# A chunked state-space scan on one core: three kinds of element-wise steps moved from GpSimd to VectorE

## The chip, the cores and the metric

The kernel runs on one core of a Trainium2 chip. The metric is the device time of one execution in microseconds; of several runs the median counts. The core's engines work side by side, each through its own queue in order: TensorE (PE in the profile, its weight loads PEld) multiplies matrices, VectorE (DVE) and ScalarE (ACT) do element-wise work, GpSimd (POOL) does element-wise work and issues some DMAs, SyncE (SP) issues DMAs.

## What is computed

One step of a hybrid decoder layer, for a prompt of 1024 positions and for 8 sequences that each decode one position. The layer projects the normalized input, runs a short causal convolution, a Mamba-2 scan in chunks of 128 positions and a pooling branch, projects back, and ends with a convolutional feed-forward block. The change touches the scan, the decode step of the scan's state, and the grouped norm behind it. The reference of the scan, cut down:

```python
acum = jnp.cumsum(dtc * a.reshape(G, R), axis=2)
decay = jnp.exp(jnp.where(causal, diff, -jnp.inf))
cb = jnp.einsum('bclgn,bcsgn->bclsg', cc, bc)
mix = cb[..., None] * decay * dtc[:, :, None]
y_diag = jnp.einsum('bclsgr,bcsgrp->bclgrp', mix, xc)
chunk_states = jnp.einsum('bclgn,bclgr,bclgrp->bcgrpn', bc, decay_to_end * dtc, xc)
chunk_decay = jnp.exp(acum[:, :, -1])
h = chunk_decay * h + chunk_states          # from chunk to chunk
y_off = jnp.einsum('bclgn,bcgrpn,bclgr->bclgrp', cc, h_in, jnp.exp(acum))
y = y_diag + y_off
```

Behind it come `y = (y + d_skip * x) * silu(z)` and a root-mean-square norm over each of four channel groups.

## The kernel before

Channels lie on the 128 partitions and positions along the free dimension. Every large product is made of three matmuls, since weights and inputs are split into a high and a low part: ScalarE makes a weight tile's high part (L140), and VectorE or GpSimd the low part (L141). A projection tile is a run of such matmuls in three column blocks (L159 to L161).

The scan has 24 heads, done in two halves of 12 (`q` = 0 and 1), each over 8 chunks (`c`). Here they are called the first and the second scan. Neither runs alone: the function `between`, called at each column block of a projection, hands out the scan's steps at a set rate, so the first scan lies between the matmuls of the projections that yield the second half's inputs, and the second between those of the gates. The order on each engine is then set by a scheduler that places the instructions by its own estimates of their durations.

One scan step `c` is made of three functions:

- `decay` loads the cumulated decays by DMA into `mix` and `ce`, clamps `mix` on VectorE (L538), and takes 12 exponentials of `mix` and one of `ce` on ScalarE (all at L188, a helper's line). Then `ce` is multiplied by C (L553): this is C with its exponentials, 128x768 elements, for every chunk but the first.
- `turn` transposes B and x on TensorE (L565, L574), multiplies B by C (L571), copies x to `xd` (L575), masks the product to `cb` (L576), scales `xd` for the state (L578) and multiplies `mix` by `cb` (L583, two instructions of 128x768), these four on VectorE.
- `apply` computes the chunk's state on TensorE (L597), multiplies the old state by its decay (L606, 128x384) and adds the two on VectorE (L610), multiplies `mix` with `xd` (L620) and `ce` with the old state (L630) on TensorE, and adds the skip on VectorE (L638).

One PSUM bank, `pM`, serves both the state product and the next transposition of B, so L565 waits for L610. The buffers of `mix`, `ce` and the state are doubled.

The decode step of a tile (`sample_tile`, L653 to L682) runs on GpSimd alone: it loads a state of 128x512 (L666), updates it (L670 to L673), stores it (L674) and reduces it with C by six halving additions (L675, L680). Of its 12 tiles, three are handed out between the two scans, four within the second, five behind it. `sample` ties each to the latest decay instruction of the scan (`self.pl`, L606), so that it is issued behind it.

Gates are applied on VectorE (L698, L700). `group_norm` takes squares on ScalarE (L710, L712) and adds them (L714, 128x1056, twice per group): on GpSimd for the first two groups, which fall within the second scan, on VectorE for the other two. `group_scale` sums over partitions on TensorE (L721) and scales on VectorE (L730).

In the first scan GpSimd also makes the low parts of the projection weights (L141, `self.lo_eng`); in the second VectorE does. The convolution of a projected tile (L516, three instructions of 128x1056) is VectorE's.

Of the kernel before, what the change touches and what calls it, by code (L numbers as in the profile page):

```python
# [13 lines left out]
ALU = mybir.AluOpType  # L14
# [4 lines left out]
P = 128  # L19
# [56 lines left out]
class Kernel:  # L76
    def __init__(self, ctx, tc, d):
        self.ctx, self.tc, self.nc, self.d = ctx, tc, tc.nc, d
        nc = self.nc
        pool = lambda name, bufs=1, **kw: ctx.enter_context(tc.tile_pool(name=name, bufs=bufs, **kw))  # L80
        self.const = pool("const")
        self.wpool = pool("weights")
        self.big = pool("big", 30)
        self.dram = pool("scratch", 1, space=DRAM)

        self.cst = self.const.tile([P, NCONST], F32, name="cst")
        self.mat = self.const.tile([P, NMAT], F32, name="mat")
        self.conv_st = self.const.tile([P, 16, 35], F32, name="conv_st")
        self.ones = self.const.tile([P, P], F32, name="ones")
        nc.vector.memset(self.ones, 1.0)  # L90
        self.zero = self.const.tile([P, P], mybir.dt.bfloat16, name="zero")
        nc.vector.memset(self.zero, 0.0)
        self.eps = self.const.tile([P, 1], F32, name="eps")
        nc.gpsimd.memset(self.eps, EPS)
        self.ident = self.mat[:, M_ID : M_ID + P]
        self.uid = 0
        self.lo_eng = nc.vector
        self.hooks = []
        self.pl = None
        self.tab = self.set = None  # L100
        self.table_set(EXPLN)

# [426 lines left out]
    def decay(self, q, c):  # L529

        nc = self.nc
        h0 = 12 * q
        mix = self.ph.tile([P, 12, P], F32, tag="mix", name=self.nm("mix"), bufs=2)
        src = lambda h, n, p: self.acd[c : c + 1, h * P : (h + n) * P].partition_broadcast(p)
        nc.sync.dma_start(mix.rearrange("p r l -> p (r l)"), src(h0, 12, P))
        hs = c * NH + h0

        nc.vector.scalar_tensor_tensor(  # L538
            out=mix, in0=self.acl[:, hs : hs + 12].unsqueeze(2).broadcast_to([P, 12, P]), scalar=80.0, in1=mix,
            op0=ALU.subtract, op1=ALU.max,  # L540
        )
        ce = None
        if c > 0:
            ce = self.ph.tile([P, 6, P], F32, tag="ce", name=self.nm("ce"), bufs=2)
            for g in range(2):
                rows = slice(64 * g, 64 * g + 64)
                nc.sync.dma_start(ce[rows].rearrange("p r l -> p (r l)"), src(h0 + 6 * g, 6, 64))
        for r in range(12):
            self.tables(mix[:, r], mix[:, r], AF.Exp, bias=self.acl[:, hs + r : hs + r + 1], scale=-1.0)
        if c > 0:  # L550
            self.tables(ce, ce, AF.Exp, scale=-1.0)
            cc = self.ctl[q][:, c * P : (c + 1) * P]
            nc.gpsimd.tensor_tensor(out=ce, in0=ce, in1=cc.unsqueeze(1).broadcast_to([P, 6, P]), op=ALU.mult)  # L553
        return mix, ce

    def turn(self, q, c, mix):
# [31 lines left out]
    def apply(self, q, c, mix, ce, xd, bT):  # L588

        nc = self.nc  # L590
        cols = slice(c * P, (c + 1) * P)
        h = self.hst.get(q)
        halves = [slice(0, 64), slice(64, 128)]
        pys = [self.bank("pY") for _ in range(2)]
        pst = self.bank("pM")
        for g, rows in enumerate(halves):
            nc.tensor.matmul(  # L597
                pst[rows, :384], bT[:, rows], xd[:, 1, 6 * g : 6 * g + 6].rearrange("p r x -> p (r x)"),
                start=True, stop=True,
            )  # L600
        h1 = self.ph.tile([P, 384], F32, tag="h", name=self.nm("h"), bufs=2)
        if c == 0:
            nc.scalar.activation(h1, pst[:, :384], AF.Copy)
        else:
            by_head = lambda t: t.rearrange("p (r x) -> p r x", x=64)
            self.pl = nc.gpsimd.tensor_tensor(  # L606
                out=by_head(h1), in0=by_head(h),
                in1=self.cd[:, c, q].unsqueeze(2).broadcast_to([P, 6, 64]), op=ALU.mult,
            ).ins
            nc.vector.tensor_tensor(out=h1, in0=h1, in1=pst[:, :384], op=ALU.add)  # L610
        self.hst[q] = h1
        if c == NCH - 1:
            nc.sync.dma_start(self.d["ssm_p"][q], h1)

        for g in range(2):
            for i in range(3):
                o = slice(i * P, (i + 1) * P)
                for j, out in enumerate(halves):
                    r = 6 * g + 2 * i + j
                    nc.tensor.matmul(  # L620
                        pys[g][out, o], xd[:, 0, r, :], mix[:, r, :], start=(i == 0), stop=(c == 0 and i == 2),
                        skip_group_check=True,
                    )

        for i in range(3 if c > 0 else 0):
            o = slice(i * P, (i + 1) * P)
            for j, out in enumerate(halves):
                r = 2 * i + j
                for g, rows in enumerate(halves):
                    nc.tensor.matmul(  # L630
                        pys[g][out, o], h[rows, r * 64 : (r + 1) * 64], ce[rows, r, :], start=False, stop=(i == 2),
                        skip_group_check=True,
                    )
        for g in range(2):
            for i in range(3):
                k = 6 * q + 3 * g + i
                t = self.xs[k][:, cols]
                nc.vector.scalar_tensor_tensor(  # L638
                    out=t, in0=t, scalar=self.c("dsk", k), in1=pys[g][:, i * P : (i + 1) * P],
                    op0=ALU.mult, op1=ALU.add,  # L640
                )
# [65 lines left out]
    def group_norm(self, g):  # L707
        nc = self.nc
        sq = [self.short(SW, "sq") for _ in range(2)]
        nc.scalar.activation(sq[0], self.xs[3 * g], AF.Square)  # L710
        for i in range(1, 3):
            nc.scalar.activation(sq[1], self.xs[3 * g + i], AF.Square)  # L712
            eng = nc.gpsimd if g < 2 else nc.vector
            eng.tensor_tensor(out=sq[0], in0=sq[0], in1=sq[1], op=ALU.add)  # L714
        self.later(2, lambda: self.group_scale(g, sq))

    def group_scale(self, g, sq):
# [36 lines left out]
    def ssd_phase(self):  # L754
        nc, d = self.nc, self.d
# [18 lines left out]
        def ssd_tasks(q):  # L774
            dec, trn = {}, {}

            def start():
                dec[0] = self.decay(q, 0)

            def step(c):  # L780
                if c >= 0:
                    self.apply(q, c, *dec.pop(c), *trn.pop(c))
                if c + 1 < NCH:
                    trn[c + 1] = self.turn(q, c + 1, dec[c + 1][0])
                if c + 2 < NCH:
                    dec[c + 2] = self.decay(q, c + 2)
                if c == -1 and q == 0:
                    self.sample_bc(q)
                if q == 1 and c in (0, 2, 4, 6):
                    sample(3 + c // 2)  # L790

            queue.append(start)
            for c in range(-1, NCH):
                queue.append(lambda c=c: step(c))

        def sample(i):
            with self.behind(self.pl):
                self.sample_tile(i // 6, i)

        self.lo_eng = nc.gpsimd  # L800
        for n in range(1, 6):
# [8 lines left out]
        for i in range(3):  # L810
            queue.append(lambda i=i: sample(i))
# [808 lines left out]
```

## Time and profile before

| | us |
|---|---|
| median of 3 runs | 1403.05 |
| the runs | 1397.98, 1403.05, 1403.52 |
| the profiled execution | 1399.9 |
| its span on the core | 1398.1 |

The profile is of one execution. Its page gives each engine's busy time and share of the span; a table of stretches gives the same for parts of the span, with the mean clock that TensorE was granted as a share of full speed. In the list of waits a row reads: the engine and line that waited, the engine and line that ended the wait, the total in us, how many times, the longest. In a timeline a row has start and duration in us, engine, line, operation, output and inputs, shape, and in brackets the idle time ahead of it with what ended it. A row of a group has the number of instructions, their busy time in us, the mean duration in ns, and the engine's idle time ahead of them.

### The profile page before, as it was taken

Reading aid. Unit: us, or ns where it says so; the run is one execution under the profiler, and the core shown is the slowest. Engines: PE = TensorE matmul, PEld = TensorE weight load, DVE = VectorE, ACT = ScalarE, POOL = GpSimd, SP = SyncE. Lnnn points to the kernel's source line nnn. Section 1 sums busy time; section 2 is a strip of 40 time slices with the busy share of each in tenths; the row PEclk is TensorE's granted clock in tenths of the full one; section 3 lists DMA queues with packets and bytes.
Section 4 is the critical chain, followed back from the end, with each engine's and each line's share of the span. In section 5 each row is a group of like instructions: output and inputs, shape, how many; then the busy total and the mean of one; then the engine's idle time right before and its main releaser. Section 6 shows DMA issues by size and latency. Waiting matters only on the chain.

```text
span 1398.1 us, 26823 instructions
## 1 busy us (share of the span) xinstructions
PE 1359.6 (97%) x10360; PEld 1312.8 (94%) x10360; DVE 986.9 (71%) x1501; ACT 701.3 (50%) x1408; POOL 496.8 (36%) x656
## 2 busy tenths in 40 slices
PE   8999999988999999999979999999999999999997
PEld 7799879977799999999979999999999999999997
DVE  6575899588864685755789867776776787567743
ACT  6346774655645451312447545554555465444451
POOL 4233466888578202122321222221222223214122
PEclk9999999999999999999989999999999999999999
DMA  7031235252331258665586877777777869657513
GB/s 250 1 109 39 87 121 173 81 162 98 95 105 63 73 187 280 224 199 187 151 199 151 210 202 197 199 191 200 176 179 199 204 214 324 225 180 238 179 54 121
DMA packets 117819, 228.08 MB, mean 163 GB/s; under 512 B 19884, under 2 KB 37116, under 8 KB 117692
## 3 DMA queue, kind: packets, MB, share of 16 engines
q1 hardware_dynamic: 73772, 130.21, 29.7%
q0 software_dynamic: 27056, 70.22, 20.0%
q10 hardware_dynamic: 16864, 25.95, 5.6%
q8 instruction: 81, 1.33, 0.4%
q14 instruction: 46, 0.38, 0.1%
HBM read 169.64 MB, written 45.15 MB: 154 GB/s over the span
## 4 chain that ended last, share of the span: by engine, by line
PE 82%; DVE 7%; DMA 3%; POOL 3%; issue 3%; ACT 2%; DVEq 0%; SPq 0%; POOLq 0%; ACTq 0%
PE g L1120 30%; PE g L1307 15%; PE g L160 10%; PE g L161 10%; PE g L159 10%; DVE wop L141 1%; DVE mix L583 1%; PE pY L620 1%; DVE xd L578 1%; POOL st L680 1%; DMA s<-wup 1%; DVE xs L516 1%; DVE xs L638 1%; PE pY L630 1%; DVE mix L538 1%
## 5 line engine op out<-in xcount | busy, mean ns | idle before, releaser
L1120 PE MATMUL g<-op,wop 128*128 128x258 f32 x3696 | 448.0, 284 | 3.9 <-ACT op L1045 3.7
L1120 PEld LDWEIGHTS g<-op,wop 128*128 128x128 f32 x3696 | 446.9, 190 | 4.7 <-ACT op L1045 4.1
L140 ACT ACTIVATE wop<-raw 128x512 fp32r<-128x512 f32 (+1 forms) x208 | 125.9, 608 | 228.1 <-PE g L161 134.3
L1307 PE MATMUL g<-op,wop 128*128 128x258 f32 x1848 | 224.9, 283 | 1.6 <-ACT op L210 0.8
L159 PE MATMUL g<-hh,wop 128*128 128x344 f32 x696 | 226.3, 325 | 0.0
L160 PE MATMUL g<-hl,wop 128*128 128x344 f32 x696 | 225.6, 324 | 0.0
L161 PE MATMUL g<-hh,wop 128*128 128x344 f32 x696 | 225.1, 323 | 0.0
L1307 PEld LDWEIGHTS g<-op,wop 128*128 128x128 f32 x1848 | 222.5, 189 | 2.6 <-ACT op L210 1.0
L141 DVE TENSOR_TENSOR wop<-raw,wop 128x512 fp32r<-128x512 f32 (+1 forms) x186 | 139.2, 752 | 88.6 <-ACT wop L140 86.6
L140 ACT ACTIVATE wop<-s 128x512 fp32r<-128x512 f32 (+1 forms) x136 | 83.6, 620 | 140.2 <-PE g L1307 51.9
L159 PEld LDWEIGHTS g<-hh,wop 128*128 128x128 f32 x696 | 132.5, 190 | 1.2 <-issue 1.1
L161 PEld LDWEIGHTS g<-hh,wop 128*128 128x128 f32 x696 | 132.3, 190 | 1.2 <-issue 1.2
L160 PEld LDWEIGHTS g<-hl,wop 128*128 128x128 f32 x696 | 132.2, 190 | 0.5 <-issue 0.4
L1100 POOL DMA_DIRECT2D s<-s x44 | 37.7, 857 | 249.8 <-DMA s<-wup 114.4
L1202 DVE SCALAR_TENSOR_TENSOR acc<-u,cst,acc 128x1048 f32<-128x1048 f32 x88 | 115.2, 1309 | 12.2 <-ACT acc L1200 10.6
L141 DVE TENSOR_TENSOR wop<-s,wop 128x512 fp32r<-128x512 f32 (+1 forms) x136 | 92.2, 683 | 36.3 <-ACT wop L140 33.9
L1180 DVE TENSOR_TENSOR u<-u,g 128x258 f32<-128x258 f32 (+2 forms) x176 | 58.2, 355 | 71.5 <-PE g L1120 64.1
L1177 ACT ACTIVATE u<-g 128x258 f32<-128x258 f32 (+2 forms) x220 | 69.6, 340 | 70.2 <-PE g L1120 70.0
L161 PE MATMUL g<-yh,wop 128*128 128x344 f32 x288 | 92.0, 319 | 0.0
L160 PE MATMUL g<-yl,wop 128*128 128x344 f32 x288 | 91.9, 320 | 0.0
L159 PE MATMUL g<-yh,wop 128*128 128x344 f32 x288 | 91.8, 319 | 0.0
L1277 POOL DMA_DIRECT2D g<-td x77 | 41.1, 539 | 122.9 <-DVE op L211 69.4
(276 smaller groups left out, 2279.8 us busy)
## 6 DMA issues: line engine op xcount, KB each, us to landing
s<-wup SPq DMA_DIRECT2D x88, 256.0 KB, 3.1
g<-td POOLq DMA_DIRECT2D x77, 258.0 KB, 4.6
raw<-wup SPq DMA_DIRECT2D x66, 256.0 KB, 3.9
raw<-win SPq DMA_DIRECT2D x58, 256.0 KB, 2.6
mix<-acd SPq DMA_DIRECT2D x16, 768.0 KB, 4.5
td<-acc ACTq DMA_DIRECT2D x22, 516.0 KB, 6.2
s<-wup POOLq DMA_DIRECT2D x44, 256.0 KB, 5.4
s<-s POOLq DMA_DIRECT2D x44, 256.0 KB, 3.7
```

What stands on the lines that cost most here:

```text
L140: self.nc.scalar.activation(hi, raw[:, :w], AF.Copy)
L141: lo_eng.tensor_tensor(out=lo, in0=raw[:, :w], in1=hi.bitcast(F32), op=ALU.subtract)
L159: nc.tensor.matmul(ps[:, :n], wh, xh[:, sl], start=(first and k == 0), stop=False)
L160: nc.tensor.matmul(ps[:, :n], wh, xl[:, sl], start=False, stop=False)
L161: nc.tensor.matmul(ps[:, :n], wl, xh[:, sl], start=False, stop=(final and k == last))
L1100: nc.gpsimd.dma_start(t, raw[acc] if acc in raw else w[acc][j], accum_op=ALU.add)
L1120: nc.tensor.matmul(out, a, b, start=(p in OPENS and j == 1), stop=(j == 12), skip_group_check=True)
L1177: a = nc.scalar.activation(out, ps[:, s], AF.Copy, scale=-1.0 if p in ("p5", "p4") else 1.0)
L1180: nc.vector.tensor_tensor(out=out, in0=out, in1=ps[:, s], op=op)
L1202: nc.vector.scalar_tensor_tensor(out=acc, in0=u[:, k : k + FW], scalar=self.c("fw", 3 * n + k), in1=acc, op0=ALU.mult, op1=ALU.add)
L1277: self.loaded = self.nc.gpsimd.dma_start(st[:, j], self.td[i + j][ROW[p]]).ins
L1307: self.pe = nc.tensor.matmul(out, a, b, start=(s == 0 and i == 0 and j == 0), stop=(s == len(PIECES) - 1 and i == nk - 1 and j == 2),).ins
```

## The change

Three kinds of instructions that GpSimd ran move to VectorE: C with its exponentials (L553, 14 instructions), the decay of the state (L606, 14) and the additions of squares of the first two groups (L714, 4). GpSimd keeps the decode steps, and they are no longer tied to the scan. Lines of the changed kernel are 1 to 4 lower than those named above.

```diff
@@ decay
-            nc.gpsimd.tensor_tensor(out=ce, in0=ce, in1=cc.unsqueeze(1).broadcast_to([P, 6, P]), op=ALU.mult)
+            nc.vector.tensor_tensor(out=ce, in0=ce, in1=cc.unsqueeze(1).broadcast_to([P, 6, P]), op=ALU.mult)
@@ apply
-            self.pl = nc.gpsimd.tensor_tensor(
+            nc.vector.tensor_tensor(
                 out=by_head(h1), in0=by_head(h),
                 in1=self.cd[:, c, q].unsqueeze(2).broadcast_to([P, 6, 64]), op=ALU.mult,
-            ).ins
+            )
             nc.vector.tensor_tensor(out=h1, in0=h1, in1=pst[:, :384], op=ALU.add)
@@ group_norm
-            eng = nc.gpsimd if g < 2 else nc.vector
-            eng.tensor_tensor(out=sq[0], in0=sq[0], in1=sq[1], op=ALU.add)
+            nc.vector.tensor_tensor(out=sq[0], in0=sq[0], in1=sq[1], op=ALU.add)
@@ ssd_phase
         def sample(i):
-            with self.behind(self.pl):
-                self.sample_tile(i // 6, i)
+            self.sample_tile(i // 6, i)
```

GpSimd's queue in the second scan, at its second chunk, before (the names are tiles: `st` and `stt` the decode state, `dx` and `xs` its input and output, `ce` C, `h` the scan's state):

```order
L682 TENSOR_TENSOR xs_931<-xs_931,dx_2661 128x8
L666 DMA st_2999<-st_ssm 128x512
L672 TENSOR_TENSOR st_2999<-st_2999,dA 128x512
L553 TENSOR_TENSOR ce_2843<-ce_2843,xs_1561 128x768
L673 TENSOR_TENSOR stt_3002<-st_2999,stt_3002 128x512
L606 TENSOR_TENSOR h_3048<-h_2932,cd 128x384
```

and in the changed kernel:

```order
L681 TENSOR_TENSOR xs_931<-xs_931,dx_2661 128x8
L665 DMA st_2999<-st_ssm 128x512
L669 TENSOR_TENSOR dx_3275<-dtS,xs_1129 128x8
L680 TENSOR_SCALAR xs_1129<-xs_1129,cst 128x8
L671 TENSOR_TENSOR st_2999<-st_2999,dA 128x512
L672 TENSOR_TENSOR stt_3002<-st_2999,stt_3002 128x512
```

C and the decay are gone from between the decode step's instructions, and two short ones of the next decode step have moved up.

VectorE's queue in the middle of the first scan, before, from the last skip of one chunk to the state's addition of the next (`mix`, `xd` and `h` as above, `pM` the state product):

```order
L638 SCALAR_TENSOR_TENSOR xs_1228<-xs_1228,cst,pY_1846 128x128
L578 TENSOR_TENSOR xd_1883<-xd_1883,wd 128x768
L583 TENSOR_TENSOR mix_1751<-mix_1751,cb_1884 128x768
L538 SCALAR_TENSOR_TENSOR mix_1906<-acl,mix_1906 128x1536
L610 TENSOR_TENSOR h_1984<-h_1984,pM_1981 128x384
```

and in the changed kernel:

```order
L637 SCALAR_TENSOR_TENSOR xs_1228<-xs_1228,cst,pY_1846 128x128
L582 TENSOR_TENSOR mix_1751<-mix_1751,cb_1884 128x768
L605 TENSOR_TENSOR h_1984<-h_1850,cd 128x384
L577 TENSOR_TENSOR xd_1883<-xd_1883,wd 128x768
L582 TENSOR_TENSOR mix_1751<-mix_1751,cb_1884 128x768
L552 TENSOR_TENSOR ce_1754<-ce_1754,xs_717 128x768
L537 SCALAR_TENSOR_TENSOR mix_1906<-acl,mix_1906 128x1536
L515 SCALAR_TENSOR_TENSOR xs_2087<-u_1840,cst,xs_2087 128x1056
L609 TENSOR_TENSOR h_1984<-h_1984,pM_1981 128x384
```

The decay and C now stand in VectorE's row, C behind the two mix products of its chunk, the decay ahead of the addition that uses it.

VectorE's queue in the second scan where the first group's squares are added, before, from one chunk's scaled `xd` to the next chunk's `cb`:

```order
L578 TENSOR_TENSOR xd_3402<-xd_3402,wd 128x768
L583 TENSOR_TENSOR mix_3252<-mix_3252,cb_3403 128x768
L610 TENSOR_TENSOR h_3478<-h_3478,pM_3475 128x384
L575 COPY xd_3511<-pT_3517 128x384
L576 TENSOR_TENSOR cb_3512<-pT_3517,mat 128x128
```

and in the changed kernel (`z` is a gate, `sq` the squares):

```order
L577 TENSOR_TENSOR xd_3402<-xd_3402,wd 128x768
L582 TENSOR_TENSOR mix_3252<-mix_3252,cb_3403 128x768
L697 TENSOR_TENSOR xs_931<-xs_931,z_3189 128x1024
L699 TENSOR_TENSOR xs_931<-xs_931,z_3189 128x8
L712 TENSOR_TENSOR sq_3357<-sq_3357,sq_3358 128x1056
L552 TENSOR_TENSOR ce_3428<-ce_3428,xs_1561 128x768
L609 TENSOR_TENSOR h_3478<-h_3478,pM_3475 128x384
L574 COPY xd_3511<-pT_3517 128x384
L712 TENSOR_TENSOR sq_3357<-sq_3357,sq_3358 128x1056
L575 TENSOR_TENSOR cb_3512<-pT_3517,mat 128x128
```

A gate, both additions of squares and C now stand ahead of this `cb`.

TensorE's matmuls are the same in number; the scheduler has placed the chunks of the two scans anew between the projections, the last chunk of the first scan somewhat later than before. From the end of the second scan on, the orders are alike.

More of the change, by code (lines that the diff above doesn't have):

```diff
@@ L98, in __init__ @@
         self.hooks = []
-        self.pl = None
         self.tab = self.set = None
```

## The prediction

> **What bounds the kernel now.** I read the page first, then the busy time by stretches, then what TensorE waited for, and last the timelines of VectorE and GpSimd around the longest waits.
>
> ```profile
> span 1398.1 us, 26823 instructions
> PE 1359.6 (97%) x10360; PEld 1312.8 (94%) x10360; DVE 986.9 (71%) x1501; ACT 701.3 (50%) x1408; POOL 496.8 (36%) x656
> ```
>
> TensorE is busy for 97% of the span, so a change elsewhere pays only where TensorE is held up. The change touches two scans, each woven into projections. In the stretches the columns are busy time of TensorE, its weight loads, VectorE, ScalarE and GpSimd, then the clock that TensorE was granted.
>
> ```profile
> 140.00:240.00 100.00, 95.88 (x834) 84.14 (x833) 92.87 (x134) 68.37 (x151) 57.30 (x46) 0.98 0.41 130
> 280.00:400.00 120.00, 108.15 (x838) 93.14 (x837) 94.78 (x137) 68.88 (x142) 87.60 (x90) 0.91 0.38 116
> ```
>
> Busy time times clock is the work done at full clock: in the first scan 95.88 × 0.98 leaves 6.0 us lost of 100, in the second 108.15 × 0.91 leaves 21.6 us lost of 120. These 27.6 us are nearly all that can be won. VectorE is idle for 7.1 us of the first stretch and 25.2 us of the second: the first scan is close to being bound by VectorE, the second is not. TensorE's waits between 130 and 480 us:
>
> ```profile
> PE pY L630 <- POOL ce L553: 5.8, 2, 4.7
> PE pM L565 <- DVE h L610: 3.7, 4, 1.9
> PE pM L597 <- DVE xd L578: 3.5, 2, 3.2
> PE pT L571 <- DVE cb L576: 2.8, 1, 2.8
> ```
>
> Each long wait is followed by a stretch at a lower granted clock, which costs about as much again:
>
> ```profile
> 290.00:300.00 10.00, 8.13 (x58) 6.29 (x59) 4.27 (x13) 2.93 (x8) 9.41 (x16) 0.68 0.26 93
> 330.00:340.00 10.00, 8.57 (x43) 7.61 (x45) 8.52 (x11) 6.01 (x16) 6.26 (x5) 0.66 0.17 54
> 370.00:380.00 10.00, 6.77 (x46) 4.85 (x46) 9.62 (x7) 6.34 (x12) 7.71 (x9) 0.75 0.25 80
> 380.00:390.00 10.00, 10.00 (x80) 8.96 (x80) 9.32 (x16) 4.95 (x8) 4.33 (x4) 0.91 0.03 5
> ```
>
> Two of these waits begin on GpSimd. The 4.7 us wait is C (L553) queued behind a decode step (L672), which itself waited for its load:
>
> ```profile
> 288.63 1.42 POOL L672 TENSOR_TENSOR st<-st,dA 128x512 f32<-128x512 f32 x1 [3.15 <-DMA st<-st_ssm]
> 290.01 1.80 POOL L553 TENSOR_TENSOR ce<-ce,xs 128x768 f32<-128x768 f32 x1
> 291.87 1.55 PE L630 MATMUL pY<-ce,h 64*64 64x128 f32 x12 [4.67 <-POOL ce L553]
> ```
>
> The other two start on VectorE, in instructions drawn out while GpSimd ran: a weight's low part (L141) ahead of L576, and xd (L578) ahead of L597.
>
> ```profile
> 325.37 5.26 DVE L141 TENSOR_TENSOR wop<-raw,wop 128x512 fp32r<-128x512 f32 x1
> 325.31 2.48 POOL L714 TENSOR_TENSOR sq<-sq,sq 128x1056 f32<-128x1056 f32 x1
> 371.35 4.74 DVE L578 TENSOR_TENSOR xd<-xd,wd 128x768 f32<-128x768 f32 x1
> 372.78 1.81 POOL L553 TENSOR_TENSOR ce<-ce,xs 128x768 f32<-128x768 f32 x1
> ```
>
> **What leaves GpSimd.** By group (busy time, mean ns), the first scan's two rows and the second's three:
>
> ```profile
> L553 POOL TENSOR_TENSOR ce<-ce,xs 128x768 f32<-128x768 f32 x7 | 18.5, 2641 | 24.2 <-ACT ce L188 24.1
> L606 POOL TENSOR_TENSOR h<-h,cd 128x384 f32<-128x384 f32 x7 | 10.2, 1459 | 11.2 <-DVE h L610 7.6 <-PE pY L630 3.6
> L553 POOL TENSOR_TENSOR ce<-ce,xs 128x768 f32<-128x768 f32 x7 | 13.8, 1968 | 10.3 <-ACT ce L188 10.3
> L606 POOL TENSOR_TENSOR h<-h,cd 128x384 f32<-128x384 f32 x7 | 7.8, 1112 | 5.8 <-DVE cb L576 3.8 <-PE pY L630 1.9
> L714 POOL TENSOR_TENSOR sq<-sq,sq 128x1056 f32<-128x1056 f32 x4 | 9.9, 2478 | 5.4 <-DMA raw<-win 5.4
> ```
>
> That is 28.7 us in the first scan and 31.5 us in the second, 60.2 us in all.
>
> **What VectorE gains.** It has instructions of the same kinds and sizes (durations min/median/max): L583 has C's shape, L610 the decay's, and L714 already runs there for the last two groups.
>
> ```profile
> L583 DVE TENSOR_TENSOR mix<-mix,cb x32: 944/958/2792, 138.4 to 387.2; 128x768 f32<-128x768 f32 x32
> L578 DVE TENSOR_TENSOR xd<-xd,wd x16: 946/960/4742, 139.2 to 386.4; 128x768 f32<-128x768 f32 x16
> L610 DVE TENSOR_TENSOR h<-h,pM x14: 540/542/556, 159.1 to 390.5; 128x384 f32<-128x384 f32 x14
> L714 DVE TENSOR_TENSOR sq<-sq,sq x4: 1258/1619/2042, 421.2 to 469.5; 128x1056 f32<-128x1056 f32 x4
> ```
>
> Undisturbed that is 7 × 0.958 + 7 × 0.542 = 10.5 us in the first scan, and the same with 4 × 1.258, 15.5 us, in the second: 26.0 us.
>
> **What VectorE gets back.** Its instructions with two inputs in SBUF run longer than their medians in the scans (the median rows of L516 and L141, then the first scan's groups, then the second's):
>
> ```profile
> L516 DVE SCALAR_TENSOR_TENSOR xs<-u,cst,xs x48: 1300/1318/2875, 81.3 to 266.0; 128x1056 f32<-128x1056 f32 x48
> L141 DVE TENSOR_TENSOR wop<-raw,wop x186: 547/686/5256, 228.1 to 1342.0; 128x512 fp32r<-128x512 f32 x142, 128x384 fp32r<-128x384 f32 x44
> L516 DVE SCALAR_TENSOR_TENSOR xs<-u,cst,xs 128x1056 f32<-128x1056 f32 x15 | 26.1, 1741 | 0.1
> L583 DVE TENSOR_TENSOR mix<-mix,cb 128x768 f32<-128x768 f32 x15 | 17.0, 1132 | 0.8 <-ACT mix L188 0.8
> L578 DVE TENSOR_TENSOR xd<-xd,wd 128x768 f32<-128x768 f32 x8 | 10.4, 1304 | 0.0
> L583 DVE TENSOR_TENSOR mix<-mix,cb 128x768 f32<-128x768 f32 x14 | 20.1, 1439 | 0.0
> L141 DVE TENSOR_TENSOR wop<-raw,wop 128x512 fp32r<-128x512 f32 x12 | 16.1, 1347 | 2.2 <-ACT wop L140 2.2
> L578 DVE TENSOR_TENSOR xd<-xd,wd 128x768 f32<-128x768 f32 x7 | 11.4, 1622 | 0.0
> ```
>
> The excess is 15 × 0.423 + 15 × 0.174 + 8 × 0.344 = 11.7 us in the first scan, and 14 × 0.481 + 12 × 0.661 + 7 × 0.662 = 19.3 us in the second. I give the moved work its share of GpSimd's busy time there: 28.7 of 57.3, half, so 5.9 us; 31.5 of 87.6, 36%, so 6.9 us. VectorE therefore grows by 10.5 − 5.9 = 4.6 us in the first scan (7.1 idle) and by 15.5 − 6.9 = 8.6 us in the second (25.2 idle), 13.2 us together. The bounds are nothing got back, +26.0 us, and everything got back that these groups show, 26.0 − 31.0 = −5.0 us.
>
> A page weighs on just this. The Trainium skill, Perfetto Trace Analysis, § Optimizing Scalar/DVE Operations, says that offloading from a saturated VectorE, even to GpSimd, may make sense, and then that it might not help because the two share an SBUF port. By the first half the first scan would pay its whole 10.5 us; the rows, at 4.6 us, stand between the halves.
>
> **What TensorE wins.** (a) The two waits for C, 5.8 us, and the slow clock behind the first, 8.13 × 0.32 = 2.6: 8.4 us. C on VectorE stands behind the mix products of its own chunk, ahead of the matmuls that use it, so I take all of it; late next is the mix product itself. (b) The wait for L576, 2.8, with 8.57 × 0.34 = 2.9 of slow clock, is 5.7 us. L141 was 4.6 us late; the moved sum of squares covers 2.48 of that, decode steps the rest, so half: 2.8 us. (c) The wait for L578, 3.5, with 6.77 × 0.25 + 10 × 0.09 = 2.6, is 6.1 us; of the 3.8 us that L578 was late C covers 1.81, so again half: 3.0 us. Together 14.2 us. The 3.7 us behind L610 I leave: VectorE's queue makes it, and that gets longer.
>
> **What comes back as new waits.** VectorE has 32.3 us of idle time for 13.2 us more work, but 7.1 of it lies where it is 93% busy, and part is time in which it waits itself. I charge 40% of the growth to TensorE: 5.2 us, between 0 (idle time takes it) and 13.2 (all on the path).
>
> C on VectorE could also wait in order for ScalarE's exponentials, and behind it stand L538, which starts the next chunk's exponentials, and L610, on which TensorE waits. On GpSimd that wait was long:
>
> ```profile
> POOL ce L553 <- ACT ce L188: 34.3, 7, 10.3
> 200.09 0.83 ACT L188 ACTIVATE ce<-ce 128x768 f32<-128x768 f32 x1
> DVE h L610 <- POOL st L680: 4.6, 2, 2.4
> ```
>
> But C's exponential (0.83 us) comes right after the chunk's mix exponentials, and VectorE's mix product (0.96 us) ahead of C waits for the last of those, so I take nothing; one full exponential in each of 14 chunks, 11.6 us, is the bound. Against it stands the last row: twice VectorE stood, 4.6 us in all, for the decay queued behind decode steps, which goes; I leave both at nothing. The decode steps, with their loads and stores on GpSimd's queue, are no longer tied to the scan and come earlier. Their readers are late gates; I take nothing. Behind 400 us all stays as it was.
>
> **The sum.** −14.2 + 5.2 = −9.0 us. The profiled execution took 1399.9 us (span 1398.1), so it would take 1390.9; the runs' median, 1403.05, lies 3.2 us above it, and against that median I predict 1394.
>
> **The rivals.** Changes within 0.5% (7.0 us) are what a measurement of this kernel can't tell from none.
>
> *The gain is given back*: all 13.2 us of VectorE's growth turn into TensorE waits, since its first stretch is 93% busy. −14.2 + 13.2 = −1.0: 1402. For it speaks the wait behind L610, already VectorE's; against it, 25.2 us of idle time in the second scan.
>
> *Slower: VectorE becomes the cycle of the scan.* Decode steps, now alone on GpSimd, fill the time that was freed at once, so VectorE's instructions stay drawn out, and all 26.0 us of new work lie on the step that TensorE waits for: 26.0 − 14.2 = +11.8: 1415. It decides once the growth is over 14.2 + 7.0 = 21.2 us, that is when less than 4.8 of the 12.8 us come back. For it: L141 and L578 also stood behind decode steps; against it: in the first scan hardly any decode runs.
>
> *Much faster: the lock.* If VectorE and GpSimd can't read at the same time, moving work takes 60.2 us of locked time away and puts back 26.0. All of the excess, 31.0 us, would go, VectorE would shrink by 5.0, and most of the 27.6 us would be won, say 20: 1383. The stretched rows speak for it; against it, only half of the excess lies under moved work. The Trainium skill, SBUF — State Buffer, § Who interferes with whom, has this rule: a VectorE instruction with two SBUF inputs and a GpSimd one that reads SBUF exclude each other, for the whole instruction; L141's 5.26 against 0.686 us agrees.
>
> **How the numbers follow.** The forecast gets 0.52 (its own range is 1387 to 1401: 0 to 10 us charged, and 2 us for the scatter of medians), given back 0.26, slower 0.12, the lock 0.10. The range 1385 to 1407 leaves out the slower rival and most of the lock, 2 in 10. Faster by over 0.5% (under 1396) is the lock and most of the forecast, 0.10 + 0.44; the same is 0.08 + 0.26; slower 0.12.
>
> **What would show it.** Right: no wait of L630's matmuls on GpSimd; GpSimd lighter by some 50 us; C on VectorE near 0.96 us; the second scan's loss down from 21.6 to about 12, with fewer slow-clock stretches; VectorE about 13 us busier. Wrong: new waits of TensorE for C or the decay on VectorE, a first scan that loses more than 6.0 us, or VectorE's instructions still at 1.4 to 1.6 us beside decode steps.

## The result, and the profile after

The changed kernel takes 1381.84 us (median of 4 runs, 1381.11 to 1386.93) against 1402.34 us of the kernel before: a ratio of 0.9876, 95% interval 0.9839 to 0.9913. That is faster by some 17 us, or 1.2%, and below the lower end of the predicted range (1385). The profiled executions, 1381.11 us after and 1399.9 before, differ by 18.8 us where the prediction's sum had 9.0.

The page after, its span and its busy times:

```profile
span 1379.3 us, 26781 instructions
PE 1347.6 (98%) x10360; PEld 1301.2 (94%) x10360; DVE 991.9 (72%) x1533; ACT 700.1 (51%) x1408; POOL 455.6 (33%) x624
```

GpSimd is lighter by 41.2 us, not by the 60.2 us that were taken from it; VectorE is busier by only 5.0 us, not by 13.2. The two stretches of the scans, columns as before:

```profile
140.00:240.00 100.00, 99.14 (x862) 87.32 (x862) 93.12 (x148) 69.12 (x153) 25.55 (x24) 1.00 0.37 121
280.00:400.00 120.00, 115.63 (x928) 101.68 (x928) 106.83 (x160) 75.06 (x152) 90.45 (x94) 1.00 0.42 129
```

The first loses 0.9 us (6.0 before), the second 4.4 us (21.6 before). The granted clock is 1.00 in both, so the stretches at a lower clock went together with the waits. In the second, GpSimd is as busy as before (90.45 against 87.60 us): decode steps fill what was freed. What TensorE still waits for between 130 and 480 us:

```profile
PE pM L564 <- DVE h L609: 3.7, 4, 2.5
PE pT L719 <- DVE sq L712: 2.7, 1, 2.7
PE pY L619 <- DVE mix L582: 0.6, 2, 0.4
PE pT L570 <- DVE cb L575: 0.4, 1, 0.4
PE pM L596 <- DVE xd L577: 0.4, 2, 0.2
```

No wait for C is left; those for `cb` and `xd`, 2.8 and 3.5 us before, are 0.4 each. The addition to the state still costs 3.7 us in all, but not in the same place: before, all four waits lie in the first scan; after, 0.9 us of them does, and 2.9 us lie in the second. A new wait, 2.7 us, is for sums of squares. It falls at 455 us, behind the second scan, and these sums ran on VectorE before as well.

VectorE's groups that the prediction used for what comes back (busy time, mean ns), first in 140 to 240 us and then in 280 to 400 us:

```profile
L515 DVE SCALAR_TENSOR_TENSOR xs<-u,cst,xs 128x1056 f32<-128x1056 f32 x16 | 23.9, 1501 | 0.0
L582 DVE TENSOR_TENSOR mix<-mix,cb 128x768 f32<-128x768 f32 x15 | 15.8, 1052 | 0.0
L577 DVE TENSOR_TENSOR xd<-xd,wd 128x768 f32<-128x768 f32 x8 | 7.6, 946 | 0.0
L552 DVE TENSOR_TENSOR ce<-ce,xs 128x768 f32<-128x768 f32 x7 | 6.6, 949 | 0.4 <-ACT ce L187 0.4
```

```profile
L582 DVE TENSOR_TENSOR mix<-mix,cb 128x768 f32<-128x768 f32 x14 | 15.4, 1102 | 0.0
L140 DVE TENSOR_TENSOR wop<-raw,wop 128x512 fp32r<-128x512 f32 x16 | 13.0, 839 | 5.2 <-ACT wop L139 5.2
L577 DVE TENSOR_TENSOR xd<-xd,wd 128x768 f32<-128x768 f32 x7 | 8.8, 1258 | 0.0
```

C takes 949 ns on VectorE, as forecast from L583. By the prediction's own medians the excess is 16 × 0.183 + 15 × 0.094 = 4.3 us in the first scan (11.7 before) and 14 × 0.144 + 16 × 0.153 + 7 × 0.298 = 6.6 us in the second (19.3 before).

To see where the time went I set marks at the starts of the projection matmuls 480, 1152, 1584 and 1811 of the trace, counted from 0 (only those that write a tile `g`): the first scan lies between the first two, the second between the next two, and no scan beyond. The table has every kernel of this study, in us, from its profiled execution (c_back's is its slowest run, 10 us above its median).

| kernel | 480 to 1152 (first scan) | 1152 to 1584 (second scan) | 1584 to 1811 | ratio to before (95%) |
|---|---|---|---|---|
| before | 150.95 | 130.02 | 37.75 | |
| after | 146.33 | 115.45 | 37.77 | 0.9876 (0.9839–0.9913) |
| c_only | 149.11 | 128.26 | 39.60 | 0.9975 (0.9957–0.9993) |
| decay_only | 148.96 | 130.57 | 39.82 | 1.002 (0.9999–1.0041) |
| sums_only | 150.92 | 126.64 | 37.75 | 0.9968 (0.9947–0.999) |
| untied_only | 150.90 | 131.99 | 37.76 | 1.0006 (0.9984–1.0029) |
| c_back | 149.00 | 136.68 | 39.61 | 1.0011 (0.9984–1.0038) |
| decay_back | 149.13 | 137.32 | 39.61 | 1.007 (1.0049–1.009) |
| sums_back | 146.38 | 140.29 | 37.75 | 1.0038 (1.0018–1.0059) |
| before_nodecode | 149.87 | 111.28 | 37.83 | 0.9884 (0.9857–0.9911) |
| after_nodecode | 146.35 | 109.49 | 37.75 | 0.9856 (0.9823–0.989) |
| heavy_read | 146.36 | 147.13 | 47.53 | 1.0163 (1.0121–1.0206) |
| heavy_free | 146.32 | 132.40 | 61.31 | 1.0162 (1.0133–1.0191) |
| set_free | 146.34 | 110.88 | 37.75 | 1.0034 (1.0015–1.0053) |
| read_free | 146.35 | 134.32 | 37.76 | 1.0144 (1.0109–1.0179) |
| before_set | 150.92 | 115.93 | 37.76 | 0.9866 (0.9841–0.9891) |
| before_noload | 149.76 | 131.71 | 37.76 | 1.002 (1.0001–1.0038) |
| norm3 | 146.30 | 117.82 | 38.57 | 0.991 (0.9883–0.9936) |

Of the 18.8 us the first scan has 4.6 and the second 14.6. Behind the last mark both kernels take the same time within 0.1 us. In c_only, decay_only, c_back, decay_back and norm3 six matmuls for a norm's sums fall behind the third mark and not ahead of it, so their second scan is to be read as about 2 us longer (the last column of the first four is longer by as much).

Each row is one execution. In the first scan, kernels whose scan steps run on the same engines agree within 0.1 us, before_nodecode and before_noload apart, which lie some 1 us off. For the second scan there is no such check, so a few us there decide nothing.

### The profile page after: what moved, and what is told of

Read it like the earlier page. It is cut to its first block, busy times and chain, and to the rows that moved or that the text cites. A ratio compares the mean times of both kernels' runs of the same rounds, so it can differ in the third digit from the quotient of the medians.

```text
span 1379.3 us, 26781 instructions
## 1 busy us (share of the span) xinstructions
PE 1347.6 (98%) x10360; PEld 1301.2 (94%) x10360; DVE 991.9 (72%) x1533; ACT 700.1 (51%) x1408; POOL 455.6 (33%) x624
## 3 DMA queue, kind: packets, MB, share of 16 engines
q0 software_dynamic: 27056, 70.22, 20.2%
## 5 line engine op out<-in xcount | busy, mean ns | idle before, releaser
L140 DVE TENSOR_TENSOR wop<-raw,wop 128x512 fp32r<-128x512 f32 (+1 forms) x186 | 132.5, 718 | 74.0 <-ACT wop L139 73.2
L160 PEld LDWEIGHTS g<-hh,wop 128*128 128x128 f32 x696 | 131.0, 188 | 2.1 <-issue 2.0
L158 PEld LDWEIGHTS g<-hh,wop 128*128 128x128 f32 x696 | 131.0, 188 | 2.0 <-issue 1.9
L1274 POOL DMA_DIRECT2D g<-td x77 | 41.2, 539 | 122.9 <-DVE op L210 69.3
```

The source lines that it names most:

```text
L140: lo_eng.tensor_tensor(out=lo, in0=raw[:, :w], in1=hi.bitcast(F32), op=ALU.subtract)
L158: nc.tensor.matmul(ps[:, :n], wh, xh[:, sl], start=(first and k == 0), stop=False)
L160: nc.tensor.matmul(ps[:, :n], wl, xh[:, sl], start=False, stop=(final and k == last))
L1274: self.loaded = self.nc.gpsimd.dma_start(st[:, j], self.td[i + j][ROW[p]]).ins
```

## The experiments

Two theories were named before the first runs. The *queue* theory: what TensorE pays for is a step of the scan that stands in GpSimd's in-order queue behind decode steps. The *port* theory: GpSimd's reading draws VectorE's instructions out, and the gain goes with the reading that is taken away. A lesser one was *order* (the scheduler's new placing of the chunks). After the first four runs the queue theory was sharpened to the *chain*: TensorE waits for whichever of C and the decay comes last, so moving one alone pays nothing. Against it stood *additive*: each part brings its own share.

### One part of the change alone

Four kernels, each the kernel before with one of the four edits of the diff: C, the decay, the sums, or decode no longer tied.

```diff
# c_only
-            nc.gpsimd.tensor_tensor(out=ce, in0=ce, ...
+            nc.vector.tensor_tensor(out=ce, in0=ce, ...
# decay_only
-            self.pl = nc.gpsimd.tensor_tensor(
+            self.pl = nc.vector.tensor_tensor(
# sums_only
-            eng = nc.gpsimd if g < 2 else nc.vector
-            eng.tensor_tensor(out=sq[0], ...
+            nc.vector.tensor_tensor(out=sq[0], ...
# untied_only
-            with self.behind(self.pl):
-                self.sample_tile(i // 6, i)
+            self.sample_tile(i // 6, i)
```

> C alone on VectorE. Queue theory (TensorE waited because C stood in GpSimd's queue behind decode steps): the waits for C, 5.8 us with the slow clock behind them, go, and part of the wait for xd: 10 to 13 us faster. Port theory (what counts is how much GpSimd reads beside VectorE): C is 32.3 of the 60.2 us moved, so about 10 us faster, and VectorE's instructions with two inputs get shorter by about half of what they do in the full change. Order theory (the scheduler's new places for the scan's matmuls do it): anything, with no relation to the waits.

> The state's decay alone on VectorE. Queue theory: no wait of TensorE ended with the decay, so 0 to 2 us faster. Port theory: 18.0 of 60.2 us moved, about 5 to 6 us faster. Order theory: anything.

> The additions of squares of the first two groups alone on VectorE. Queue theory: half of the wait for the masked product cb with its slow clock, about 3 us faster. Port theory: 9.9 of 60.2 us moved, about 3 us faster. Order theory: anything.

> Only the tie of the decode steps to the scan is taken away; the orders of TensorE, VectorE and SyncE stay as before. Queue theory: the decode steps move ahead of C and the decay or behind them, up to 3 us either way. Port and order theory: 0.

Measured: 1397.42, 1403.38, 1397.64 and 1401.54 us beside 1401.21 of the kernel before. By their ratios the four together are worth some 0.3%, against 1.2% for the whole. Both theories had expected some 10 us or more of C alone; it brought 3.5 by its ratio. In c_only TensorE's longest wait moved, and VectorE's row beneath names the new place, the decay on GpSimd:

```profile
PE pM L565 <- DVE h L610: 13.6, 3, 8.8
```

```profile
DVE h L610 <- POOL h L606: 9.5, 1, 9.5
```

In decay_only it is C that TensorE waits for, in sums_only C too:

```profile
PE pY L630 <- POOL ce L553: 9.4, 1, 9.4
PE pM L565 <- DVE h L610: 7.5, 4, 3.6
```

```profile
PE pY L630 <- POOL ce L553: 9.8, 2, 9.1
```

The two scans behave differently. In the first, where little decode runs, the parts nearly add up: C alone takes 1.8 us off, the decay alone 2.0, both 4.6. In the second no part alone reaches 4 us of the 14.6, and C alone brings nothing once the 2 us of the moved matmuls are counted. Untying the decode steps does nothing, as predicted.

### One part taken back

The kernel after, with one of the three on GpSimd again (the first three edits, reversed).

> The full change with C back on GpSimd. Chain theory: TensorE waits for C again, at least 9 us in all, and most of the gain is gone: 0 to 6 us faster than before. Port theory: 27.9 of the 60.2 us are still moved: 9 us faster.

> The full change with the decay back on GpSimd. Chain theory: VectorE waits for the decay behind decode steps and TensorE for VectorE (L565), as in the run with C alone: 3 to 8 us faster than before. Port theory: 42.2 of the 60.2 us are still moved: 13 us faster.

> The full change with the additions of squares of the first two groups back on GpSimd, so C and the decay moved together. Chain theory (TensorE's step waits for whichever of C and the decay comes last off GpSimd's queue, so neither alone pays): 13 to 17 us faster than before, though the two alone gave 3.8 us faster and 2.2 us slower. Additive theory (each part pays its own): 2 us faster at most. Port theory (by the share of GpSimd's time taken away): 16 us faster, which doesn't part it from the chain here.

Measured: 1402.33, 1409.44 and 1405.92 us beside 1401.28 of before: any one of the three left behind loses the whole gain. No theory had said so. The chain had 13 to 17 us won in sums_back, where C and the decay moved together, 3 to 8 in decay_back and 0 to 6 in c_back; the port theory had 9 us or more won in each. The wait stands at the step that stayed. In c_back:

```profile
PE pY L629 <- POOL ce L552: 22.5, 3, 10.5
```

In decay_back TensorE's row, and the row of VectorE under it:

```profile
PE pM L564 <- DVE h L609: 19.2, 6, 8.0
```

```profile
DVE h L609 <- POOL h L605: 25.0, 5, 8.3
```

In sums_back TensorE waits for ScalarE to copy a gate's product out of PSUM. ScalarE was itself held up: its next square, which overwrites an input of the first addition, had to wait for that addition on GpSimd, and the copy stood behind the square in ScalarE's queue.

```profile
PE g L158 <- ACT z L692: 19.1, 1, 19.1
```

```profile
ACT sq L711 <- POOL sq L713: 25.5, 1, 25.5
```

That a late step in GpSimd's queue holds TensorE up is what the queue theory said; the sums, which are no step of the scan, do it too. But it tells where the late step stands, not what made GpSimd late.

### Without the decode arithmetic

Both kernels with the arithmetic of the first seven decode tiles left out; their states are only loaded and stored.

```diff
         def sample(i):
-            self.sample_tile(i // 6, i)
+            self.sample_copy(i)      # load st, store st
```

> The kernel before, with the arithmetic of the first seven decode tiles left out (their state is loaded and stored, nothing is computed from it); C, the decay and the sums stay on GpSimd. Queue theory: what TensorE waited for was never the time of these three steps on GpSimd, but the decode steps queued ahead of them; without those the steps run as soon as they are ready, and most of the gain of the whole change appears, -15 to -22 us against before, with the waits behind L553 and L606 under 2 us together after 280 us. Port theory: the gain goes with GpSimd's reading time taken from beside VectorE; the change took 60.2 us and won 20, the decode tiles have some 90 us (their 90.45 us of busy time in 280 to 400 after the change), so -30 us. Rival that the three steps are themselves too slow on GpSimd: under 6 us are won.

> The kernel after the change, with the arithmetic of the first seven decode tiles left out in the same way: what these still cost. Queue theory: nothing of the chain stands behind them any more; only the gates' 5 us or less of waits in the second scan can go, 0 to -4 us against after (1378 to 1382). Port theory: VectorE gets back the 16.6 us by which its work between 265 and 385 us was drawn out, and with it -8 us or more.

Measured: 1380.74 and 1377.13 us beside 1396.75. The second stretch in before_nodecode, and the same in after_nodecode:

```profile
280.00:400.00 120.00, 120.00 (x955) 107.00 (x954) 94.26 (x149) 77.29 (x156) 49.81 (x50) 0.95 0.40 122
```

```profile
280.00:400.00 120.00, 120.00 (x965) 107.70 (x965) 97.41 (x160) 77.14 (x154) 24.29 (x27) 1.00 0.33 102
```

TensorE is busy throughout in both. The clock of 0.95 in the first is no slow stretch: that execution shows 0.94 or 0.95 from start to end. So C, the decay and the sums on GpSimd hold nobody up in the second scan unless decode runs beside them. By the marks, decode costs the second scan 130.02 − 111.28 = 18.74 us before the change and 115.45 − 109.49 = 5.96 us after it: 12.8 of its 14.6 us are a lower price of the same decode. Both theories had the sign. The sizes, −16 us against before and −3 (by the ratios) to −5 us (by the medians) against after, are nearer the queue theory's than the −30 and −8 of the port theory.

### More decode work in the kernel after

The two big multiplies of the first seven decode tiles are issued four times; TensorE's and VectorE's orders stay as they were. In heavy_free, those tiles also take their input from scratch and write to scratch, so that no gate waits for them (the decode tokens' outputs are left out).

```diff
# heavy_read
+        for _ in range(4 if i < 7 else 1):
             nc.gpsimd.tensor_tensor(out=tmp, in0=bb, in1=bcast(dx[:, 0]), op=ALU.mult)
...
+        for _ in range(4 if i < 7 else 1):
             nc.gpsimd.tensor_tensor(out=st, in0=tmp, in1=cc, op=ALU.mult)
# heavy_free, also
-        xt = self.xs_samp(self.xs[i])
+        xt = self.xs_samp(self.xs[i]) if i >= 7 else self.dtS[:, i, :]
...
```

> The full change, with two of the decode step's multiplications (128x512, two inputs in SBUF) done four times each instead of once in the first seven tiles, with the same result; the orders of TensorE and VectorE stay those of the full change. GpSimd reads about 30 us more within the second scan, as much as the change took away there. Port theory: VectorE's instructions are drawn out again, and 8 to 12 us of the gain are lost. Chain theory: no scan step stands behind them, so 0 to 3 us are lost.

> The kernel after, with the two big multiplies of the first seven decode tiles issued four times as in the run before, but these tiles read and write scratch in place of the decode tokens of x, so that no gate waits for them (those tokens' outputs are left out). It parts the two causes of that run's 1423.8 us. Port theory: GpSimd's reading alone draws VectorE's work out by some 33 us in the second scan, against 16.6 in the kernel after, and TensorE pays half or more of the difference: 1390 us or more. Queue theory: nearly all of the 42 us were gates waiting for late decode tiles; without them 1381 to 1385 us.

Measured: 1423.82 and 1419.2 us. heavy_read lost 42 us where the theories had 0 to 12; its gates waited for late decode tiles too. Without gates behind them the extra reads still cost 132.40 − 115.45 = 17.0 us inside the second scan, though no step of the scan is on GpSimd any more. That the queue theory can't explain: it had 1381 to 1385 us. The rest of heavy_free's loss lies behind the scan, where a gate waited 22.7 us for the next decode tiles, which were not freed:

```profile
DVE xs L702 <- POOL xs L684: 28.1, 3, 22.7
```

### Reading against writing, in the kernel after

Two kernels in which no decode tile at all touches the decode tokens of x (those outputs are left out). read_free has the multiplies four times, set_free six memsets beside each, in place of the repeats.

```diff
# set_free
+        for _ in range(6 if i < 7 else 0):
+            nc.gpsimd.memset(tmp, 0.0)
...
+        for _ in range(6 if i < 7 else 0):
+            nc.gpsimd.memset(st, 0.0)
# both
-        xt = self.xs_samp(self.xs[i])
+        xt = self.dtS[:, i, :]
...
```

> The kernel after, with six memsets of 128x512 beside each of the two big multiplies of the first seven decode tiles, and no decode tile touching the decode tokens of x (their outputs are left out), so that nothing waits for decode. GpSimd is as busy as in the next run. Port theory: writes alone take nothing from VectorE: the mark behind the second scan (the 1584th projection matmul, 380.6 us after the change) stays within 380 to 384, the whole 1376 to 1384 us. If the load of GpSimd's queue counts by itself: the mark at 390 or later.

> The same as the run before, but with the two multiplies issued four times in place of the memsets; no decode tile touches the decode tokens of x, so that the 22.7 us which a gate waited for a late tile in the run before last of this kind are gone too. Port theory: the mark behind the second scan comes at 395 to 400 us, as there (397.7), and the whole at 1394 to 1402 us. Queue theory: 1376 to 1384 us, as with the memsets.

Measured: 1406.13 and 1424.03 us. Both have a weight load 26 to 31 us late behind 440 us, which was not foreseen and spoils the totals; it was not followed up. The second scan, ahead of that, is clean: 110.88 us with the writes, 134.32 us with the reads, 23.4 us apart. The mark behind it comes at 375.2 and 399.5 us, where the port theory had 380 to 384 and 395 to 400. The stretch of set_free and that of read_free:

```profile
280.00:400.00 120.00, 118.75 (x957) 106.55 (x957) 103.13 (x161) 76.25 (x153) 110.71 (x129) 1.00 0.36 115
```

```profile
280.00:400.00 120.00, 104.20 (x808) 88.30 (x807) 115.49 (x147) 67.32 (x140) 110.48 (x98) 0.93 0.34 106
```

GpSimd is busy for 110.7 and 110.5 us, TensorE for 118.75 at full clock and 104.20 at 0.93. VectorE shows the reason; of each kernel the mix products and `xd` in 265 to 385 us (set_free, then read_free):

```profile
L582 DVE TENSOR_TENSOR mix<-mix,cb 128x768 f32<-128x768 f32 x16 | 16.4, 1027 | 0.0
L577 DVE TENSOR_TENSOR xd<-xd,wd 128x768 f32<-128x768 f32 x8 | 8.8, 1098 | 0.0
```

```profile
L582 DVE TENSOR_TENSOR mix<-mix,cb 128x768 f32<-128x768 f32 x16 | 20.2, 1263 | 1.7 <-ACT mix L187 1.7
L577 DVE TENSOR_TENSOR xd<-xd,wd 128x768 f32<-128x768 f32 x8 | 11.7, 1463 | 0.0
```

The same instructions take 1263 and 1463 ns beside the reads, 1027 and 1098 beside the writes. Where the inputs lie matters. Of two VectorE instructions of the same size, the state's decay (L605) has both inputs in SBUF, and the addition to it (L609) has one in PSUM. In 265 to 385 us, set_free, then read_free (durations in ns, min/median/max):

```profile
L605 DVE TENSOR_TENSOR h<-h,cd x7: 541/546/604, 282.2 to 366.1; 128x384 f32<-128x384 f32 x7
L609 DVE TENSOR_TENSOR h<-h,pM x7: 537/541/555, 287.1 to 370.2; 128x384 f32<-128x384 f32 x7
```

```profile
L605 DVE TENSOR_TENSOR h<-h,cd x6: 544/820/1615, 286.7 to 364.2; 128x384 f32<-128x384 f32 x6
L609 DVE TENSOR_TENSOR h<-h,pM x6: 539/540/543, 295.1 to 378.7; 128x384 f32<-128x384 f32 x6
```

Beside the reads the addition keeps its time and the decay doesn't. With the reads VectorE is busy for 115.5 of 120 us, and it has become what TensorE waits for: the waits of 15.8 us between 265 and 405 us all end with VectorE, against 1.2 us in set_free. A long queue on GpSimd costs nothing by itself once nothing of the scan stands in it. One limit: a memset is also shorter than a multiply (0.53 us against 1.04 at the least, in before), so these two kernels do not part reading from the length of GpSimd's instructions.

### Reading against queueing, in the kernel before

before_set has memsets in place of the big arithmetic of the first seven decode tiles, long enough to keep GpSimd busy. before_noload keeps the arithmetic and leaves out the loads of the states, on which GpSimd waits.

```diff
# before_set, i < 7, in place of the two multiplies by B and decay, the addition, the product with C and the halvings
+            2 x memset(tmp), 3 x memset(st), 3 x memset(tmp), [store], 9 x memset(st)
# before_noload
-        nc.gpsimd.dma_start(st, d["st_ssm"][i])
+        if i >= 7:
+            nc.gpsimd.dma_start(st, d["st_ssm"][i])
...
-        nc.gpsimd.tensor_tensor(out=st, in0=st, ...
+        nc.gpsimd.tensor_tensor(out=st, in0=st if i >= 7 else tmp, ...
```

> The kernel before, with the big arithmetic of the first seven decode tiles replaced by memsets that take GpSimd about as long (17 of 128x512, some 9 us a tile by the 128x384 memset's 0.42 us) but read nothing; these tiles' states and tokens are left out. GpSimd's queue ahead of C, the decay and the sums stays as long as it was, its reading goes. Queue theory: the waits behind L553 and L606 stay, 1396 to 1403 us, as before. Port theory: it is GpSimd's reading that cost, and the gain of leaving the decode's arithmetic out altogether (1380.7) appears here too: 1379 to 1386 us. In between: each has its share.

> The kernel before, with the states of the first seven decode tiles not loaded: the same multiplies, adds and halvings read as many elements, from a product already on the chip in place of the loaded state (these tiles' states and tokens are left out). GpSimd's reading stays, its waits for the loads of the states (1.9 and 3.2 us between 268 and 290 us, the second right ahead of the late C at 290.0) go; the other loads of these tiles (B and C of the decode tokens) stay. Queue theory: C and the decay are no longer late behind those waits, 1381 to 1388 us, as with the memsets (1383.3). Port theory: the reading was the price, 1394 to 1402 us.

Measured: 1383.25 us beside 1401.6, and 1400.72 beside 1399.22. The stretch in before_set, where GpSimd is busier than before (101.49 against 87.60 us), and two of its groups in 265 to 385 us:

```profile
280.00:400.00 120.00, 116.48 (x925) 102.91 (x926) 97.17 (x148) 75.33 (x152) 101.49 (x112) 0.99 0.38 120
```

```profile
L680 POOL MEMSET st<- 128x512 f32 x44 | 23.1, 526 | 1.5
L553 POOL TENSOR_TENSOR ce<-ce,xs 128x768 f32<-128x768 f32 x7 | 19.1, 2727 | 4.8 <-DVE xs L638 4.8
```

Writes in decode's place win what leaving it out wins, within 5 us (115.93 against 111.28), although C itself takes 2.7 us there. Reads without the loads win nothing. In before_noload TensorE waited for C again:

```profile
PE pY L630 <- POOL ce L553: 9.6, 2, 9.2
```

C was late behind the rest of a decode tile, with instructions that were drawn out (the addition takes 2.66 us here, 1.29 in the tile ahead of it):

```profile
285.92 2.66 POOL L674 TENSOR_TENSOR stt<-st,stt 128x512 f32<-128x512 f32 x1
288.88 0.61 POOL L675 DMA_DIRECT2D ssm_s<-stt  x1 [0.30 <-POOL stt L674]
289.51 1.28 POOL L676 TENSOR_TENSOR st<-stt,bc 128x512 f32<-128x512 f32 x1
290.87 1.99 POOL L681 TENSOR_TENSOR st<-st 128x256 f32<-128x256 f32 x4
292.81 1.80 POOL L553 TENSOR_TENSOR ce<-ce,xs 128x768 f32<-128x768 f32 x1
```

So the price stays without the waits for the states' loads, and goes with writes in place of the decode's arithmetic. Something stays open: both kernels also moved C in GpSimd's queue (in before_set ahead of a tile's load, in before_noload behind nearly a whole tile). That the loads had no share before is therefore not shown, and how much of the 18.7 us came from C and the decay standing late in the queue, and how much from VectorE drawn out, is not parted.

### A later scaling of the norms

The new 2.7 us wait is for sums of squares, so norm3 issues a group's scaling one slot later. The text below puts that wait into the second scan; it lies at 455 us, behind it.

```diff
-        self.later(2, lambda: self.group_scale(g, sq))
+        self.later(3, lambda: self.group_scale(g, sq))
```

> The kernel after, with a group norm's scaling issued three slots behind its sums and not two. The one wait of TensorE for sums left in the second scan (2.7 us, L719 behind L712) should go. If nothing else moves: -1 to -3 us against after, 1379 to 1381 us. If the later scaling makes the output projections behind it late, or holds the short buffers that gates need: the same or up to +10 us.

Measured: 1384.4 us, 0.991 (0.9883 to 0.9936), no better than the change. The wait for the squares is gone, but those for `xd` and the mix product grew from 0.4 and 0.6 us to 1.7 and 1.0, and the second scan is 2.4 us longer, with six matmuls fewer in it. No version of this study beats the changed kernel with all of its outputs.

## Why the prediction was wrong

The direction and the two scans as the place were right. The sum was half of what came, and it had nothing for the first scan, which won 4.6 us. Step by step:

- **(a) C, all of it: right in the whole change only.** No wait for C is left. But the sum adds up the waits as if each could go by itself. In c_only, which moves C alone, the wait for C went too, a wait of up to 8.8 us behind the decay came in its place, and 3.5 us were won and not 8.4.
- **(b) and (c), "again half": wrong.** The prediction counted which GpSimd instruction lay beside L141 and L578 and gave the decode steps the other half. Both waits fell to 0.4 us, with their slow clock: about 11 us went where 5.8 were counted. Decode steps still run beside those instructions, but draw them out less.
- **What VectorE gets back: mis-sized.** By shares of GpSimd's busy time it was 12.8 us. By the same groups and medians it is 11.7 − 4.3 = 7.4 us in the first scan and 19.3 − 6.6 = 12.7 us in the second, 20.1 us. VectorE so grows by 26.0 − 20.1 = 5.9 us and not 13.2; the page has 5.0. The share of busy time was the wrong measure: in the second stretch GpSimd is as busy as before, and the excess fell to a third.
- **"The 3.7 us behind L610 I leave": wrong, and the total of 3.7 is luck.** Before, all of it lies in the first scan. After, TensorE's waits for this addition are, between 130 and 260 us and then between 265 and 405 us:

```profile
PE pM L564 <- DVE h L609: 0.9, 1, 0.9
```

```profile
PE pM L564 <- DVE h L609: 2.9, 3, 2.5
```

"VectorE's queue makes it, and that gets longer" held for the count of instructions. But those of the first scan were drawn out less, so 2.8 us of the wait went there, and with it a stretch of 3.4 us at half clock (at 160 us before), worth 1.7. That comes to 4.5 of the first scan's 4.6 us. The count isn't exact: c_only lost the slow stretch too and 2.2 us of this wait, and won only 1.8 us there; why is open.
- **"I charge 40% of the growth", 5.2 us: too much.** In the second scan 2.9 us came, behind L609; no wait for C or the decay on VectorE came.
- **The cost of nothing for untying decode: right** (untied_only). VectorE's 4.6 us of waits for the decay, also left at nothing, lay in the second scan; after the change VectorE waits for no decay there.

With (b) and (c) whole, the second scan wins 8.4 + 5.7 + 6.1 = 20.2 us, less 4.3 us of waits that are left or new there: 15.9, against 14.6 by the marks. The first scan adds its 4.6. Together that is 20.5, against 18.8 measured.

The nearest rival was the lock, 1383, at a chance of 0.10. Its time was right, and its reason in part: GpSimd's reading instructions have a price beside VectorE's instructions with two inputs, which set_free and read_free show. The Trainium skill, SBUF — State Buffer, § Who interferes with whom, limits the lock to a GpSimd instruction that reads SBUF, not one that only writes it; the 23.4 us between the two kernels agree. But VectorE did not shrink by 5.0 us, as the rival had it, and against it the prediction held that "only half of the excess lies under moved work". That was true, and no argument: the excess that lay beside decode went down too.

The theory with which the experiments began, the queue, is half of the story. Shown is: any one of the three steps on GpSimd beside decode costs the whole gain of the second scan; without decode's arithmetic none of them costs it; and it is reading instructions, not time in the queue, that cost where no step of the scan is queued.

## What to carry to other kernels

If steps that others wait for are split over two engines that draw each other out, try moving all of them, and do not judge by one: here each of three moves alone brought 0.3% or less, and all three 1.2%. What contention costs is not read from the other engine's busy time; put a write of the same length in place of a read and see what goes. Where a part of a wait lies beside work that stays, cost it at nothing and at the whole, and keep both ends in the range. A wait with the same total before and after need not be the same wait: look where it lies.

## What the runs showed of the hardware

After the change two of the decode step's instructions on GpSimd are drawn out more than before. Of before and then of after, between 140 and 400 us, the multiply with B and the decay of the decode state (mean ns in the second number):

```profile
L671 POOL TENSOR_TENSOR stt<-bc,dx 128x512 f32<-128x512 f32 x8 | 9.4, 1178 | 6.1 <-DMA bc<-bcd 3.9 <-DMA bcd<-bcs 2.2
L672 POOL TENSOR_TENSOR st<-st,dA 128x512 f32<-128x512 f32 x7 | 10.5, 1507 | 6.1 <-DMA st<-st_ssm 6.1
```

```profile
L670 POOL TENSOR_TENSOR stt<-bc,dx 128x512 f32<-128x512 f32 x9 | 20.1, 2235 | 12.2 <-DMA bcd<-bcs 6.9 <-DMA ssm_s<-stt 4.0 <-DMA bc<-bcd 1.2
L671 POOL TENSOR_TENSOR st<-st,dA 128x512 f32<-128x512 f32 x7 | 15.7, 2247 | 15.4 <-DMA st<-st_ssm 15.4
```

The same instructions went from 1178 and 1507 to 2235 and 2247 ns, one of them to 5.29 us. That is a part only of why GpSimd became lighter by 41.2 us and not by 60.2: by summed durations all decode steps together grew from 157.4 to 165.2 us, and other instructions grew as well, the copies `u<-fst` far behind the scans from 27.5 to 32.9 us. A memset of 128x512 on GpSimd took 521 to 526 ns on average in before_set's groups between 265 and 400 us, beside VectorE's scan work: it is not drawn out. Why VectorE's instructions are drawn out less after the change, with GpSimd as busy, is open; that they now stand closer together was only argued, not tried.
